# Attention on one core: first pair's transposes in another order, value units numbered from four, last head normalised in one piece

## The chip, the cores and the metric

The kernel runs on one core of a Trainium2 chip, as one launch. The metric is the device time in microseconds (us), the median of several runs. A core has five engines that run side by side, each with its own instruction stream, and that wait for one another through semaphores: TensorE (PE in the profile; its weight loads are PEld), VectorE (DVE), ScalarE (ACT), GpSimd (POOL) and SyncE (SP), which issues DMAs. TensorE writes its results into PSUM, from which ScalarE and VectorE read.

## The reference

```python
def reference(q, k, v):                      # each [8, 8, 512, 64], float32
    scale = 1.0 / np.sqrt(q.shape[-1])
    scores = np.einsum('bhqd,bhkd->bhqk', q, k) * scale
    scores = scores - scores.max(axis=-1, keepdims=True)
    attn = np.exp(scores)
    attn = attn / attn.sum(axis=-1, keepdims=True)
    return np.einsum('bhqk,bhkd->bhqd', attn, v).astype(np.float32)
```

These are 64 independent heads of softmax attention, with 512 queries, 512 keys and 64 dimensions each.

## The kernel before

**Tiling.** Heads go in pairs, 32 of them (`g` from 0 to 31). A head's keys and queries are cut into four chunks of 128. A block `(g, c, h)` is the scores of key chunk `c` of head `h` of pair `g` against all 512 queries; it is computed transposed, keys on the partitions, so that exp(scores) can be the stationary operand of the second product without another transpose. Two blocks make a group: one PSUM buffer `st` of two banks (three such buffers rotate), one exp of 128x1024 on ScalarE into an fp16 tile `pt`. The last two blocks are groups of their own (127 and 128). No maximum is subtracted.

**A pair's way.** k, q and v come by DMA from SyncE's queue. GpSimd casts them to fp16 (`cast_qk`, `cast_v`). Eight TensorE transposes of a pair (`transposes`) go into a PSUM bank, and VectorE copies the bank to `tqk` (`copy`). Two matmuls per group make the scores (`scores`), which run in half of the array's rows each. The second product is cut into units: one unit is a chunk of 128 queries of one head, four matmuls of 65 columns that accumulate over the four key chunks. The 65th column of v is one, so that the sum of the exps comes out beside the result (`values`). Seven units share one PSUM bank. When a bank is full, VectorE takes the reciprocals of the sums and multiplies (`normalise`), into an SBUF ring of 56 units, and SyncE writes each complete head out.

**Raised groups.** Six groups are not given to ScalarE: VectorE computes their exp by integer and polynomial steps (`raise_`, which reads `st`, and six `pass_` steps that read SBUF only).

**Two PSUM banks for transposes and values.** Tags `x0` and `x1` are shared by the transposes' banks and the units' banks, so whichever asks next has to wait until VectorE has read the older one.

**Order.** It is written out beforehand: `Plan` walks through time with a cost for each step (`SLOT`, `EXP`, `NORM` and so on) and emits a list of steps; the kernel then issues them in that order under a manual schedule. On TensorE, `step_pe` chooses between scores, transposes and value units; `HURRY` is the amount of exp work queued at ScalarE below which scores are issued at once. On VectorE, `step_dve` takes jobs that are due (raise first, then copies and normalisings by due time), and starts a pass of a raised group where the next job is due later than the pass's length less `LATE`. Each engine executes its own stream strictly in that order.

**Opening.** Pair 0 is handled apart (`first_loads`, `first_pair`), since nothing can start until its q and k have come. Its loads and casts are cut in halves. While they come, TensorE multiplies a matrix of ones (`busy`), six times with 512 columns and three with 128. Then: q of head 0, first half, is transposed (`tp_qa`), k of head 0, first half (`tp_ka`), q's second half (`tp_qc`), k's second half (`tp_kc`); each is copied by VectorE. Two more matmuls of ones, then the scores of the first group in two halves of 256 queries (`st_0a`, `st_0b`), k of head 1 transposed (`tp_kb`), group 1's scores, q of head 1 (`tp_qb`), one matmul of ones with 256 columns, group 2's scores. From group 3 on the plan takes over.

**End.** The last head of pair 31 is not in units: as each of its four key chunks has its exp, `last_values` adds that chunk to all four query chunks. Before the change these four lie in two places, two query chunks each (a bank and one of the three score buffers), the exp of the last block is cut in two halves of 256 queries, and each half is normalised and written out by itself, one through SyncE's queue and one through ScalarE's.

Of the kernel before, what the change touches and what calls it, by code (L numbers as in the profile page):

```python
# [8 lines left out]
FP32 = mybir.dt.float32  # L9
# [7 lines left out]
class Plan:  # L17
# [10 lines left out]

    SLOT, EXP, EXP_DONE, EXP_FIXED = 216, 853, 1085, 51
# [4 lines left out]
    RAISE, PASSES, LATE = 1216, (867, 822, 1400, 1400, 1400, 1372), 500  # L34
    HURRY = 1100
    STEP = 5

    def __init__(self, groups, pairs, first):
# [14 lines left out]
        self.units = 0  # L53
# [74 lines left out]

    def values(self, t):
        if self.head is None:  # L130
# [5 lines left out]
            if self.units % 7 == 0 and self.bank(t) is None:  # L136
                return False
# [5 lines left out]
        if self.units % 7 == 0:  # L143
            n = self.bank(t)
            if n is None:
                return False
            self.banks[n] = 1e9
            self.bank_v = n
        self.note(t, "values", g, h, part, self.units, self.bank_v)
        self.full(t, self.V_UNIT)  # L150
        self.units += 1
        last = (g, h) == (self.pairs - 1, 1)
        if self.units % 7 == 0 and not last:
            self.ready.append((self.pe + self.TO_DVE, "norm", (self.units - 7, 7, self.bank_v)))
# [66 lines left out]
def kernel(  # L221
# [128 lines left out]
    def scores(m, on_dve):  # L350
# [19 lines left out]
        if m == len(groups) - 1:  # L370
            pt2 = ppool.tile([P, 2, S], FP16, tag="pt", name="pt_last")
            blocks[grp[0]] = (pt[:, 0, :], pt2[:, 0, :])
            for n, t in enumerate((pt, pt2)):
                q2 = slice(256 * n, 256 * n + 256)
                nc.scalar.activation(out=t[:, 0, q2], in_=st[:, 0, q2], func=EXP, scale=scale)
            return
# [58 lines left out]
    def normalise(u, n):  # L435
        o = os[u // 7]
        rc = opool.tile([P, 7, 1], FP32, tag="rc", name=f"rc_{u}")
        nc.vector.reciprocal(out=rc[:, 0:n], in_=o[:, 0:n, D : D + 1])  # L438
        nc.vector.tensor_tensor(  # L439
            out=ring[:, u % NU : u % NU + n, :],  # L440
            in0=o[:, 0:n, 0:D],
# [9 lines left out]
    def values(g, h, y, u, bank):  # L451
# [5 lines left out]
        if u % 7 == 0:  # L457
# [10 lines left out]
    def last_values(c, bank):  # L468


        if c == 0:
            last["o"] = [
                ps_x.tile([P, 7, D + 1], FP32, tag=f"x{bank}", name="o_last_0"),
                ps_st.tile([P, 2, S], FP32, tag="st", name="o_last_1")[:, 0, 0 : 2 * D + 2].rearrange(
                    "p (n d) -> p n d", n=2
                ),
            ]
            last["ob"] = [opool.tile([P, 2, D], FP32, tag="obl", name=f"obl_{n}") for n in range(2)]
        for n in range(2):
            o, ob = last["o"][n], last["ob"][n]  # L480
            for x in range(2):
# [177 lines left out]
```

## Time and profile before

The profile is one execution of the program.

| | before |
|---|---|
| median of 5 runs | 124.22 us (124.0 to 124.27) |
| the profiled execution | 124.27 us, of which the span is 122.5 us |
| ScalarE busy | 114.4 us (93% of the span), 128 instructions |
| TensorE busy | 108.1 us (88%), 1562 matmuls |
| VectorE busy | 98.2 us (80%), 159 instructions |
| GpSimd busy | 70.5 us (58%) |
| DMA | 33.81 MB, 276 GB/s on average |

The span is cut into 40 equal slices of about 3.06 us; a digit is the busy share of a slice in tenths:

```profile
PE   7979698899899899989899798899988899898960
DVE  0455989799979989989999988978998699798460
ACT  4499999999999999999999999999999999999950
DMA  3899999999999969989999999999999933222234
```

Three lines are at or near nine tenths through the middle, so the shares alone don't tell which engine sets the pace. A row of costliest groups reads: line of the kernel, engine, operation, written tile <- read tiles with their shapes, count | busy us in total, mean ns of one | idle us of the engine just before them, and what ended most of it. A timeline row reads: start in us, us, engine, line, operation, tiles, count, and in brackets the idle time before it and what ended it. Rows of the timeline join several instructions of a kind; their ends overlap[...].

### The profile page before, as it was taken

The page shows a single profiled execution, that of the slowest core. Times are in us where ns is not written, and L with a number is a line of the kernel's source. Part 1 is how long each engine was busy: PE and PEld are TensorE (multiplying, and loading weights), DVE is VectorE, ACT ScalarE, POOL GpSimd, SP SyncE. Part 2 cuts the span into 40 slices and gives each one's busy share as a digit, 9 for nine tenths or more (in the row PEclk, how much of TensorE's full clock was granted, in tenths as well). Part 3 has the DMA queues.
Part 4 walks back from the last instruction along what each step waited for, and adds up shares of the span by engine and source line. Part 5 has one row for each costly group of instructions (what it writes and reads, how often), then busy time and mean ns, then how long its engine had stood idle before and what let it go on. Part 6 is the DMA issues. An engine that isn't in the chain of part 4 may idle for free.

```text
span 122.5 us, 3961 instructions
## 1 busy us (share of the span) xinstructions
PE 108.1 (88%) x1562; PEld 67.1 (55%) x1562; DVE 98.2 (80%) x159; ACT 114.4 (93%) x128; POOL 70.5 (58%) x113
## 2 busy tenths in 40 slices
PE   7979698899899899989899798899988899898960
PEld 2446265555565556565466555466645475565640
DVE  0455989799979989989999988978998699798460
ACT  4499999999999999999999999999999999999950
POOL 3269779999694635877967745476584690000000
PEclk9999999999999999999999999999999999999999
DMA  3899999999999969989999999999999933222234
GB/s 108 282 350 382 385 377 383 382 325 282 365 316 318 296 213 296 326 280 315 331 360 312 292 335 321 280 314 375 323 289 340 351 100 126 86 92 88 93 126 128
DMA packets 35602, 33.81 MB, mean 276 GB/s; under 512 B 2688, under 2 KB 35584, under 8 KB 35584
## 3 DMA queue, kind: packets, MB, share of 16 engines
q1 hardware_dynamic: 35152, 33.24, 82.1%
q10 hardware_dynamic: 432, 0.33, 0.8%
q8 instruction: 12, 0.20, 0.7%
q14 instruction: 6, 0.05, 0.2%
HBM read 25.17 MB, written 8.39 MB: 274 GB/s over the span
## 4 chain that ended last, share of the span: by engine, by line
ACT 54%; PE 27%; issue 14%; DVE 2%; ACTq 0%
ACT pt L377 54%; PE st L365 10%; PE o L460 10%; PE tp L339 3%; PE st_0a L516 3%; DVE tqk L344 1%; PE st L551 1%; DVE ring L439 1%; DVE obl L497 0%; DVE qt L594 0%; PE tp_qb L546 0%; PE tp_qc L546 0%; PE tp_qa L546 0%; PE st_0a L551 0%; PE tp_kb L540 0%
## 5 line engine op out<-in xcount | busy, mean ns | idle before, releaser
L377 ACT ACTIVATE pt<-st 128x1024 f16<-128x1024 f32 (+1 forms) x119 | 108.9, 1271 | 0.1
L365 PE MATMUL st<-tqk 64*128 64x512 f16 x248 | 47.8, 384 | 6.8 <-ACT pt L377 4.7
L460 PE MATMUL o<-vp,pt 128*128 128x65 f16 x1008 | 47.8, 195 | 2.0 <-ACT pt L377 1.9
L460 PEld LDWEIGHTS <-pt 128*128 128x128 f16 x1008 | 37.6, 98 | 19.0 <-issue 14.7
L322 POOL CAST qkp<-k 128x512 f16<-128x512 f32 x31 | 21.7, 699 | 24.3 <-DMA k<-in_k_dram 13.6
L314 POOL CAST vp<-v 128x512 f16<-128x512 f32 x32 | 27.3, 853 | 0.9 <-DMA v<-in_v_dram 0.7
L346 DVE COPY tqk<-tp 128x1024 f16<-128x1024 f16 x30 | 20.6, 688 | 5.8 <-PE tp L339 5.5
L322 POOL CAST qkp<-q 128x512 f16<-128x512 f32 x30 | 22.4, 748 | 3.2 <-DMA q<-in_q_dram 2.7
L365 PEld LDWEIGHTS <-tqk 64*128 64x128 f16 x248 | 12.9, 93 | 19.9 <-issue 11.6
L439 DVE TENSOR_TENSOR ring<-o,rc 128x448 f32<-128x448 f32 x36 | 22.5, 624 | 1.2
L339 PE MATMUL tp<-ident,qkp 128*128 128x128 f16 x248 | 19.7, 220 | 0.5 <-DVE ring L439 0.4
L339 PEld LDWEIGHTS <-qkp 128*128 128x128 f16 x248 | 14.1, 98 | 7.6 <-issue 4.8
L426 DVE SCALAR_TENSOR_TENSOR y<-y,m 128x1024 f32<-128x1024 f32 x12 | 15.7, 1308 | 0.0
L438 DVE RECIPROCAL rc<-o 128x7 f32<-128x7 f32 x36 | 7.2, 200 | 7.6 <-PE o L460 7.1
L426 DVE SCALAR_TENSOR_TENSOR pt<-y,e 128x1024 f16<-128x1024 f32 x6 | 8.4, 1403 | 0.0
L426 DVE SCALAR_TENSOR_TENSOR y<-m 128x1024 f32<-128x1024 f32 x6 | 8.2, 1358 | 0.0
L391 DVE TENSOR_SCALAR z<-st 128x1024 uint32<-128x1024 f32 x6 | 7.3, 1221 | 0.5 <-PE st L365 0.2
L404 DVE TENSOR_SCALAR m<-z 128x1024 uint32<-128x1024 uint32 x6 | 5.5, 909 | 0.0
L415 DVE TENSOR_SCALAR e<-z 128x1024 uint32<-128x1024 uint32 x6 | 4.5, 754 | 0.0
L516 PE MATMUL st_0a<-const-bfloat16-1.0 128*128 128x512 bf16 (+1 forms) x11 | 3.5, 482 | 0.8 <-PEq L643 0.8
L526 DVE CAST q<-q 128x128 f16<-128x128 f32 x1 | 0.2, 227 | 3.3 <-DMA q<-in_q_dram 3.3
L528 ACT ACT_TABLE_LOAD x1 | 1.3, 1283 | 1.7 <-PEq L643 1.7
(47 smaller groups left out, 20.8 us busy)
## 6 DMA issues: line engine op xcount, KB each, us to landing
out_dram<-ring SPq DMA_DIRECT2D x63, 128.0 KB, 3.9
k<-in_k_dram SPq DMA_DIRECT2D x31, 256.0 KB, 4.7
q<-in_q_dram SPq DMA_DIRECT2D x31, 256.0 KB, 4.9
v<-in_v_dram SPq DMA_DIRECT2D x27, 256.0 KB, 5.2
v<-in_v_dram SPq DMA_DIRECT2D x10, 128.0 KB, 4.6
k<-in_k_dram ACTq DMA_DIRECT2D x2, 128.0 KB, 2.8
q<-in_q_dram SPq DMA_DIRECT2D x2, 128.0 KB, 2.6
out_dram<-obl ACTq DMA_DIRECT2D x1, 64.0 KB, 1.6
```

The costliest lines, as they stand in the source:

```text
L314: nc.gpsimd.tensor_copy(out=vps[g % NV][:, :, :, 0:D], in_=raw[g]["v"][:, :, :, :])
L322: eng.tensor_copy(out=t[:, n].rearrange("p i (h d) -> p h i d", h=2), in_=raw[g][name][:, :, :, :],)
L339: nc.tensor.transpose(tps[g][:, n, i, :], qkp[g][:, n, i, :], ident)
L346: nc.vector.tensor_copy(out=tqk[g][:, :, :], in_=tps.pop(g).rearrange("p n i c -> p n (i c)"))
L365: nc.tensor.matmul(st[:, x, :], kc, qc, start=True, stop=True)
L377: nc.scalar.activation(out=pt[:, 0:size, :], in_=st[:, 0:size, :], func=EXP, scale=scale)
L391: nc.vector.tensor_scalar(out=r["z"][:, :, :], in0=r["st"][:, :, :], scalar1=scale * 1.4426950408889634 * 2.0**23, scalar2=(127 + SHIFT) * ...
L426: nc.vector.scalar_tensor_tensor(out=r["pt"][:, :, :] if n == 3 else r["y"][:, :, :], in0=mant if n == 0 else r["y"][:, :, :], scalar=QUAR ...
L438: nc.vector.reciprocal(out=rc[:, 0:n], in_=o[:, 0:n, D : D + 1])
L439: nc.vector.tensor_tensor(out=ring[:, u % NU : u % NU + n, :], in0=o[:, 0:n, 0:D], in1=rc[:, 0:n].broadcast_to([P, n, D]), op=AluOp.mult,)
L460: nc.tensor.matmul(os[u // 7][:, u % 7, :], blocks[(g, c, h)][:, y * P : (y + 1) * P], vps[g % NV][:, h, c, :], start=(c == 0), stop=(c == ...
L516: nc.tensor.matmul(dst[:, 0:n], ones[:, 0:P], ones[:, 0:n], start=True, stop=True)
```

## The change

- **Opening.** One of the three short matmuls of ones goes. The eight transposes of head 1's q (`tp_qb`) move ahead of the first scores; the transpose of k's second half (now into a part of group 1's own score buffer, as is `tp_qc`) moves from ahead of the first scores to between their two halves. The two matmuls of ones now stand ahead of group 1's scores, and the one with 256 columns ahead of group 2's is replaced by five with 128. The copies follow in the same new order; q of head 1 is copied before k of head 1.
- **Units.** Numbering starts at 4 (`FIRST_UNIT`), so the first bank holds three units, and every bank's border lies four units earlier in the order of heads. A bank also ends before the last head, so that there is a last piece of four units. `edge` says where a bank begins and ends, `normalise` takes the offset within the bank.
- **Plan's constants.** `LATE` 500 to 700, `HURRY` 1100 to 1200. With these and the units the order of all later steps comes out differently; the groups raised on VectorE were 6, 24, 43, 62, 82 and 102, and are 6, 23, 42, 62, 80 and 101.
- **End.** The last block's exp is one instruction of 512 queries. The last head's four query chunks lie in one bank, which is normalised by one reciprocal and one multiply; two DMAs still write the result, by SyncE's and ScalarE's queue.

```diff
--- before.py
+++ after.py
@@ -26,14 +26,17 @@
...
     SLOT, EXP, EXP_DONE, EXP_FIXED = 216, 853, 1085, 51
     INTO, OUT_OF = 95, 105
     TRANSPOSE, V_UNIT = 225, 130
     TO_ACT, TO_DVE, TO_PE = 275, 210, 60
     COPY, NORM, NORM_COLUMN = 700, 380, 67
-    RAISE, PASSES, LATE = 1216, (867, 822, 1400, 1400, 1400, 1372), 500
-    HURRY = 1100
+    RAISE, PASSES, LATE = 1216, (867, 822, 1400, 1400, 1400, 1372), 700
+    HURRY = 1200
     STEP = 5
+    FIRST_UNIT = 4
 
     def __init__(self, groups, pairs, first):
         self.groups, self.pairs = groups, pairs
@@ -50,7 +53,7 @@
         self.banks = [5100, 5800]
         self.todo = [(g, h) for g in range(pairs) for h in range(2)]
         self.head = None
-        self.units = 0
+        self.units = self.FIRST_UNIT
         self.member = {b: m for m, grp in enumerate(groups) for b in grp}
         self.ready = []
         self.passes = []
@@ -126,6 +129,11 @@
         chunks = (part,) if (g, h) == (self.pairs - 1, 1) else range(4)
         return max(self.exps.get(self.member[(g, c, h)], 1e9) for c in chunks)
 
+    def edge(self):
+
+        u, first = self.units, self.FIRST_UNIT
+        return u % 7 == 0 or u in (first, first + 8 * self.pairs - 4)
+
     def values(self, t):
         if self.head is None:
             for g, h in self.todo[:14]:
@@ -133,25 +141,26 @@
                     break
             else:
                 return False
-            if self.units % 7 == 0 and self.bank(t) is None:
+            if self.edge() and self.bank(t) is None:
                 return False
             self.todo.remove((g, h))
             self.head = (g, h, 0)
         g, h, part = self.head
         if t < self.wants(g, h, part):
             return False
-        if self.units % 7 == 0:
+        if self.edge():
             n = self.bank(t)
             if n is None:
                 return False
             self.banks[n] = 1e9
             self.bank_v = n
+            self.begun = self.units
         self.note(t, "values", g, h, part, self.units, self.bank_v)
         self.full(t, self.V_UNIT)
         self.units += 1
-        last = (g, h) == (self.pairs - 1, 1)
-        if self.units % 7 == 0 and not last:
-            self.ready.append((self.pe + self.TO_DVE, "norm", (self.units - 7, 7, self.bank_v)))
+        if self.edge() and (g, h) != (self.pairs - 1, 1):
+            what = (self.begun, self.units - self.begun, self.bank_v)
+            self.ready.append((self.pe + self.TO_DVE, "norm", what))
         self.head = (g, h, part + 1) if part < 3 else None
         return True
 
@@ -367,13 +376,6 @@
         if on_dve:
             raised[m] = {"st": st, "pt": pt}
             return
-        if m == len(groups) - 1:
-            pt2 = ppool.tile([P, 2, S], FP16, tag="pt", name="pt_last")
-            blocks[grp[0]] = (pt[:, 0, :], pt2[:, 0, :])
-            for n, t in enumerate((pt, pt2)):
-                q2 = slice(256 * n, 256 * n + 256)
-                nc.scalar.activation(out=t[:, 0, q2], in_=st[:, 0, q2], func=EXP, scale=scale)
-            return
         nc.scalar.activation(
             out=pt[:, 0:size, :], in_=st[:, 0:size, :], func=EXP, scale=scale
         )
@@ -433,12 +435,12 @@
         )
 
     def normalise(u, n):
-        o = os[u // 7]
+        o, x = os[u // 7], u % 7
         rc = opool.tile([P, 7, 1], FP32, tag="rc", name=f"rc_{u}")
-        nc.vector.reciprocal(out=rc[:, 0:n], in_=o[:, 0:n, D : D + 1])
+        nc.vector.reciprocal(out=rc[:, 0:n], in_=o[:, x : x + n, D : D + 1])
         nc.vector.tensor_tensor(
             out=ring[:, u % NU : u % NU + n, :],
-            in0=o[:, 0:n, 0:D],
+            in0=o[:, x : x + n, 0:D],
             in1=rc[:, 0:n].broadcast_to([P, n, D]),
             op=AluOp.mult,
         )
@@ -454,7 +456,7 @@
             return last_values(y, bank)
         if y == 0:
             heads.append((g, h, u))
-        if u % 7 == 0:
+        if u // 7 not in os:
             os[u // 7] = ps_x.tile([P, 7, D + 1], FP32, tag=f"x{bank}", name=f"o_{u // 7}")
         for c in range(NI):
             nc.tensor.matmul(
@@ -469,39 +471,31 @@
 
 
         if c == 0:
-            last["o"] = [
-                ps_x.tile([P, 7, D + 1], FP32, tag=f"x{bank}", name="o_last_0"),
-                ps_st.tile([P, 2, S], FP32, tag="st", name="o_last_1")[:, 0, 0 : 2 * D + 2].rearrange(
-                    "p (n d) -> p n d", n=2
-                ),
-            ]
-            last["ob"] = [opool.tile([P, 2, D], FP32, tag="obl", name=f"obl_{n}") for n in range(2)]
-        for n in range(2):
-            o, ob = last["o"][n], last["ob"][n]
-            for x in range(2):
-                qc = 2 * n + x
-                b = blocks[(LAST, c, 1)]
-                b = b[n] if c == NI - 1 else b
-                nc.tensor.matmul(
-                    o[:, x, :],
-                    b[:, qc * P : (qc + 1) * P],
-                    vps[LAST % NV][:, 1, c, :],
-                    start=(c == 0 and x == 0),
-                    stop=(c == NI - 1),
-                    skip_group_check=True,
-                )
-            if c < NI - 1:
-                continue
-            rc = opool.tile([P, 7, 1], FP32, tag="rc", name=f"rc_last_{n}")
-            nc.vector.reciprocal(out=rc[:, 0:2], in_=o[:, 0:2, D : D + 1])
-            nc.vector.tensor_tensor(
-                out=ob[:, :, :],
-                in0=o[:, 0:2, 0:D],
-                in1=rc[:, 0:2].broadcast_to([P, 2, D]),
-                op=AluOp.mult,
-            )
-            (nc.sync, nc.scalar)[n].dma_start(
-                out=source(out, LAST)[:, 1, 2 * n : 2 * n + 2], in_=ob[:, :, :]
+            last["o"] = ps_x.tile([P, 7, D + 1], FP32, tag=f"x{bank}", name="o_last")
+        o = last["o"]
+        for x in range(NI):
+            nc.tensor.matmul(
+                o[:, x, :],
+                blocks[(LAST, c, 1)][:, x * P : (x + 1) * P],
+                vps[LAST % NV][:, 1, c, :],
+                start=(c == 0 and x == 0),
+                stop=(c == NI - 1),
+                skip_group_check=True,
+            )
+        if c < NI - 1:
+            return
+        ob = opool.tile([P, NI, D], FP32, tag="obl", name="obl")
+        rc = opool.tile([P, 7, 1], FP32, tag="rc", name="rc_last")
+        nc.vector.reciprocal(out=rc[:, 0:NI], in_=o[:, 0:NI, D : D + 1])
+        nc.vector.tensor_tensor(
+            out=ob[:, :, :],
+            in0=o[:, 0:NI, 0:D],
+            in1=rc[:, 0:NI].broadcast_to([P, NI, D]),
+            op=AluOp.mult,
+        )
+        for n, queue in enumerate((nc.sync, nc.scalar)):
+            queue.dma_start(
+                out=source(out, LAST)[:, 1, 2 * n : 2 * n + 2], in_=ob[:, 2 * n : 2 * n + 2, :]
             )
 
     def first_loads():
@@ -530,11 +524,16 @@
         nc.scalar.copy(k16[:, 1], tk[:, 1])
         nc.gpsimd.tensor_copy(out=q16[:, 1], in_=tq[:, 1])
 
-        st0 = ps_st.tile([P, 2, S], FP32, tag="st", name="st_0a")
-        pk0 = ps_st.tile([P, 2, 8, P], FP16, tag="st", name="tp_ka")
-        pk1 = ps_st.tile([P, 2, 8, P], FP16, tag="st", name="tp_kc")
-        pq0 = ps_x.tile([P, 8, P], FP16, tag="x0", name="tp_qa")
-        pq1 = ps_x.tile([P, 8, P], FP16, tag="x1", name="tp_qc")
+        st0, pka, st1 = (
+            ps_st.tile([P, 2, S], FP32, tag="st", name=f"st_{n}") for n in ("0a", "ka", "1")
+        )
+        pqa = ps_x.tile([P, 8, P], FP16, tag="x0", name="tp_qa")
+        pqb = ps_x.tile([P, 8, P], FP16, tag="x1", name="tp_qb")
+
+        pka, pkc, pqc = pka[:, 0, :], st1[:, 0, :], st1[:, 1, :]
+        pka, pkc, pqc = (
+            t.bitcast(FP16).rearrange("p (n c) -> p n c", c=P) for t in (pka, pkc, pqc)
+        )
 
         def t_k(dst, h, j):
             nc.tensor.transpose(
@@ -561,39 +560,38 @@
 
         for n in range(6):
             busy(st0[:, 0], S)
-        for n in range(3):
+        for n in range(2):
             busy(st0[:, 0], P)
         for i in range(2):
-            t_q(pq0[:, i], 0, i)
-        nc.vector.tensor_copy(out=qt[:, 0, 0:2], in_=pq0[:, 0:2])
-        t_k(pk0[:, 0, 0], 0, 0)
-        nc.vector.tensor_copy(out=kt[:, 0, 0], in_=pk0[:, 0, 0])
+            t_q(pqa[:, i], 0, i)
+        nc.vector.tensor_copy(out=qt[:, 0, 0:2], in_=pqa[:, 0:2])
+        t_k(pka[:, 0], 0, 0)
+        nc.vector.tensor_copy(out=kt[:, 0, 0], in_=pka[:, 0])
         for i in range(2):
-            t_q(pq1[:, i], 0, 2 + i)
-        nc.vector.tensor_copy(out=qt[:, 0, 2:4], in_=pq1[:, 0:2])
-        t_k(pk1[:, 0, 0], 0, 1)
-        nc.vector.tensor_copy(out=kt[:, 0, 1], in_=pk1[:, 0, 0])
-        for n in range(2):
-            busy(st0[:, 0], P)
+            t_q(pqc[:, i], 0, 2 + i)
+        nc.vector.tensor_copy(out=qt[:, 0, 2:4], in_=pqc[:, 0:2])
+        for i in range(NI):
+            t_q(pqb[:, i], 1, i)
         pts = [ppool.tile([P, 2, S], FP16, tag="pt", name=f"pt_{m}") for m in range(3)]
         for m in range(3):
             for x, b in enumerate(groups[m]):
                 blocks[b] = pts[m][:, x, :]
         first_scores(st0, 0, 0, 0, 256, pts[0], 0, 256)
+        t_k(pkc[:, 0], 0, 1)
+        nc.vector.tensor_copy(out=kt[:, 0, 1], in_=pkc[:, 0])
+        nc.vector.tensor_copy(out=qt[:, 1], in_=pqb[:, 0:4])
         st0b = ps_st.tile([P, 2, S], FP32, tag="st", name="st_0b")
         first_scores(st0b, 0, 0, 256, 512, pts[0], 0, 256)
+        for n in range(2):
+            busy(st1[:, 1], P)
+        first_scores(st1, 0, 1, 0, S, pts[1], 0, S)
         pkb = ps_x.tile([P, 8, P], FP16, tag="x0", name="tp_kb")
         for j in range(2):
             t_k(pkb[:, j], 1, j)
         nc.vector.tensor_copy(out=kt[:, 1], in_=pkb[:, 0:2])
-        st1 = ps_st.tile([P, 2, S], FP32, tag="st", name="st_1")
-        first_scores(st1, 0, 1, 0, S, pts[1], 0, S)
-        pqb = ps_x.tile([P, 8, P], FP16, tag="x1", name="tp_qb")
-        for i in range(NI):
-            t_q(pqb[:, i], 1, i)
-        nc.vector.tensor_copy(out=qt[:, 1], in_=pqb[:, 0:4])
         st2 = ps_st.tile([P, 2, S], FP32, tag="st", name="st_2")
-        busy(st2[:, 0], 256)
+        for n in range(5):
+            busy(st2[:, 0], P)
         first_scores(st2, 1, 0, 0, S, pts[2], 0, S)
         first.update(kt=kt, qt=qt)
 
```

## The prediction, made before the changed kernel was run

> **What bounds the kernel now.** I read the table of costliest groups first, then the timeline of ScalarE (start, length, what, count, idle before it), then the timeline of all engines at both ends.
>
> ```profile
> L377 ACT ACTIVATE pt<-st 128x1024 f16<-128x1024 f32 (+1 forms) x119 | 108.9, 1271 | 0.1
> ```
>
> The exps of the planned part leave ScalarE idle for 0.1 us in 109. So TensorE's 108.1 us, VectorE's 98.2 us and the loads matter only where they make an exp late.
>
> ```profile
> 5.54 0.60 ACT L558 ACTIVATE pt<-st_0a 128x512 f16<-128x512 f32 x1 [0.97 <-PE st_0a L551]
> 6.04 0.59 ACT L558 ACTIVATE pt<-st_0b 128x512 f16<-128x512 f32 x1
> 6.51 2.17 ACT L558 ACTIVATE pt<-st 128x1024 f16<-128x1024 f32 x2
> 8.57 2.11 ACT L377 ACTIVATE pt<-st 128x1024 f16<-128x1024 f32 x2
> ...
> 114.70 2.88 ACT L377 ACTIVATE pt<-st 128x1024 f16<-128x1024 f32 x3
> 116.98 0.88 ACT L375 ACTIVATE pt<-st 128x256 f16<-128x256 f32 x1
> 117.25 0.89 ACT L375 ACTIVATE pt_last<-st 128x256 f16<-128x256 f32 x1
> ```
>
> Taken one by one, two full exps follow each other by 0.904 us in their starts but by 0.917 in their ends, and the ends are what other engines wait for. The exp that starts at 9.66 ends at 10.68, and 116 full exps later one ends at 117.09: 106.41/116 = 0.917. Only two ends in between come late, by 0.05 us (at 45.6) and 0.04 us (at 48.3). So the middle is rigid, a start may slip by its gathered lead (12.5 ns an exp) at no cost, and the change can move three things: the end at 10.68, those 0.08 us, and all that follows 117.09.
>
> The opening:
>
> ```profile
> 5.97 0.39 PE L551 MATMUL st<-qt,kt 64*128 64x512 f16 x2
> 6.29 0.41 PE L546 MATMUL tp_qb<-ident,q 128*64 128x128 f16 x8
> 6.75 0.42 DVE L594 COPY qt<-tp_qb 128x512 f16<-128x512 f16 x1 [0.38 <-PE tp_qb L546]
> 7.22 0.39 PE L551 MATMUL st<-qt,kt 64*128 64x512 f16 x2 [0.30 <-DVE qt L594]
> 8.42 0.76 DVE L344 COPY tqk<-tp 128x512 f16<-128x512 f16 x2 [0.92 <-PE tp L339]
> 9.23 0.39 PE L365 MATMUL st<-tqk 64*128 64x512 f16 x2 [0.61 <-DVE tqk L344]
> ```
>
> The fourth exp (7.65) and the sixth (9.66) start late: each waits for scores that waited for a copy on VectorE. The end:
>
> ```profile
> 116.65 1.11 PE L460 MATMUL o<-vp,pt 128*128 128x65 f16 x24
> 117.60 0.59 PE L485 MATMUL o_last<-vp,pt 128*128 128x65 f16 x14
> 117.80 0.21 DVE L438 RECIPROCAL rc<-o 128x7 f32<-128x7 f32 x1 [1.05 <-PE o L460]
> 118.04 0.62 DVE L439 TENSOR_TENSOR ring<-o,rc 128x448 f32<-128x448 f32 x1
> 118.19 0.23 PE L485 MATMUL o_last<-vp,pt_last 128*128 128x65 f16 x2
> 118.58 0.16 DVE L496 RECIPROCAL rc_last<-o_last 128x2 f32<-128x2 f32 x1
> 119.18 0.29 DVE L497 TENSOR_TENSOR obl<-o_last,rc_last 128x128 f32<-128x128 f32 x1
> 119.50 0.37 ACTq L503 DMA_DIRECT2D out_dram<-obl  x1
> 119.59 0.40 SPq L503 DMA_DIRECT2D out_dram<-obl  x1
> ```
>
> Here VectorE bounds, not the last exp: the bank of units 245 to 251 closes only with the next-to-last head, its normalising (117.80 to 118.66) stands before the last head's two pieces, and the last piece ends at 119.47.
>
> **What the Trainium skill says.** "TensorE: Matmul & The Clock Gate", Part 1, "What's actually happening": the array runs at half rate until it has been busy for one free-running window of about 3.4 us. The trace agrees: ones-matmuls of 128 columns are 107 ns apart at 3.3 us, transposes 56 ns apart at 7.8; the switch falls between 5.7 and 6.3. "Perfetto Trace Analysis", "DVE / Act Engine Instruction": a row ends when the write is acknowledged and the semaphore pushed, which is why I count exps by ends. "DMA: Bandwidth & Descriptors", "Anatomy of one DMA": about 2 us fixed for a transfer; the last two take 1.6 and 1.8 us here, so only their issue time can move.
>
> **The change, part by part.** Its waits are read from the built program's order. From the trace before: a change of matmul form costs 0.24 us from the last 128-column start to the next load (0.35 after 256 columns at half rate, 0.16 and 0.31 at full rate after 128 and 512), the end of an operation reaches TensorE 0.05 us later, and scores reach their exp 0.43 us after they start.
>
> *Opening.* One short ones-matmul goes (0.107), so tp_qa starts at 3.63 instead of 3.74 (its cast ends at 3.53). tp_ka 3.99, tp_qc 4.21 and 4.32, then the eight moved transposes (four pairs, 0.107 each) 4.42 to 4.74; their cast on GpSimd ends at 4.31, which just covers them. Out of that stretch go the kc transpose with its two form changes and two ones-matmuls. First scores 4.99 (before 5.10), first exp 5.43 (5.54). The kc transpose now stands between the halves: 5.34, then second scores 5.59 (5.29), exp 6.02 (6.04): what was gained is spent. The two ones-matmuls wait for the kc copy (5.34+0.33+0.22+0.05 = 5.94), and behind them wait the third scores: 6.16 (5.97), exp 6.58 (6.51). So far +0.07. But the long qb copy (0.42) is now made before that, and the fourth scores wait for the kb copy alone: kb 6.48 and 6.54, copy 6.79 to 7.08 (0.29), scores 7.14 (7.22), exp 7.56 (7.65). The five ones-matmuls (5 x 0.056 = 0.28) end before 7.14, beside the copy. The rest follows with it: scores 3 (7.36), pair 1's transposes 7.68 (7.76), copies until 9.10 (9.18), fifth scores 9.15, sixth exp 9.57 (9.66). **-0.08**; bounds -0.15 and +0.15, as the clock's switch is free to fall elsewhere.
>
> *Middle.* The number of exps stays, six groups are still raised on VectorE (now 6, 23, 42, 62, 80, 101), and the normalised columns stay, in 37 pieces instead of 36: one more reciprocal and multiply (about 0.4 us) on an engine idle for 20%. The first piece of three waits for units 4 to 6 (9.9+0.23), ends at 10.7, and the next units want that bank at 11.0; transposes of pair 2 are copied behind it at 10.63, no later than now. Pair 3's transposes move ahead of scores 9: these start at 12.67 and their exp, due at 13.21, could start at 13.09. HURRY and LATE shift the interleaving: a VectorE pass may now hold up a due copy or normalising by 0.7 us instead of 0.5. Below: the two small gaps go, -0.08; above: the rival below, +0.7. I take **0**, since lead hid nearly everything of this kind before.
>
> *End.* Units are now numbered from 4, so the bank of 245 to 251 closes with head 1 of pair 30, before the last pair's units: after 8 of the 24 matmuls at 116.65, last start 116.89. Its reciprocal comes at 116.89+0.23 = 117.12 (before 117.80), multiply 117.36 to 117.98. The last pair's first head gets a bank and a piece of four (estimate for 256 columns from 292 ns for 128 and 624 for 448: 0.43): about 118.10 to 118.53. New wait: the 16 o_last matmuls need the bank that the multiply frees, so they start at 118.04 instead of 117.60; nothing else is queued behind them on TensorE. They last 0.46 (15 x 0.031); the undivided exp would end at 117.58+0.49 = 118.07 (the halves: 118.13), ahead of the four that need it. Reciprocal 118.50+0.23 = 118.73, multiply 118.93 to 119.36, both DMAs at 119.40. SP's three ring DMAs (118.01, 118.40, 118.80, some 0.4 each) are out by then. Against the later of the old issues, 119.59: -0.19. TensorE can gain more: scores 128 start at 116.33, while the exp that frees their buffer ended at 116.17; up to 0.11, and pair 25's old values now stand ahead of pair 29's, which cost a wait of 0.33 us at 110.7. I take half: **-0.24**; bounds -0.4 and +0.1.
>
> *Sum:* -0.08+0-0.24 = -0.32 on the profiled 124.27 us (span 122.5, 1.77 outside), 123.95; the median of the runs is 0.05 lower: **123.90**.
>
> **Rivals.**
> - *The ends give less.* The third exp's delay stays in the chain, or the 4-unit piece pushes the last one: opening 0, end -0.1, so 124.1. For: both gains hang on steps of 0.05 to 0.1 us. Against: each copy on the chain really is shorter or earlier.
> - *ScalarE starves at raised groups (slower).* A raised group holds one of three score buffers until its first pass is done, and a delayed copy delays the next scores. At group 43 two starts slipped by 0.17+0.33 = 0.50; the lead was 0.43, so 0.05 reached the ends. Where that happens early (group 23: lead about 0.2) or twice within a few groups, 0.3 to 0.5 comes through. Two such places, +0.7: 124.6. It decides from 0.57 us on. For: LATE at 700, VectorE at nine tenths from 20 to 80. Against: five of six raised groups lost nothing.
> - *TensorE runs ahead.* With no wait at 110.7 and no gaps, the end gains 0.45 and the middle 0.08: 123.6.
>
> **How the numbers follow.** Forecast 0.55 (its own range 123.65 to 124.1), less 0.22, starved 0.15, ahead 0.08. About 0.2%, 0.25 us, is what a measurement can tell: faster is below 123.97, slower above 124.47. Faster: most of the first, the last, little of the second: 0.60. Slower: most of the starved case: 0.14. The rest, 0.26, is within. The range for 8 in 10: 123.55 to 124.35.
>
> **What would show it.** First exp at 5.43, fourth 7.56, sixth 9.57; idle before the planned exps still 0.1; the last exp's end near 118.0; o_last waiting for VectorE's multiply, and its DMAs near 119.3. Wrong if exps' ends in the middle come late by more than 0.2 in sum, or if the first 10 us gain nothing.

## The result, and the profile after

| | before | after |
|---|---|---|
| median | 124.12 us (80 runs) | 124.53 us (43 runs) |
| ratio after/before | | 1.0036 (95%: 1.0024 to 1.0048) |
| profiled execution, its span | 124.27, 122.5 us | 124.20, 122.4 us |

The change makes the kernel slower by a third of a per cent. The forecast, 123.90 us and faster, is wrong in its sign, and the result lies outside its range. Yet the steps that the forecast worked out are there in the profile. The planned exps first (columns of the costliest groups):

```profile
L379 ACT ACTIVATE pt<-st 128x1024 f16<-128x1024 f32 (+1 forms) x120 | 109.4, 1328 | 0.1
```

Idle is still 0.1 us in front of ScalarE, and exp by exp no end after the sixth comes late any more (before: 0.08 us in two places). The opening, in the timeline of ScalarE and then of TensorE:

```profile
5.22 0.60 ACT L557 ACTIVATE pt<-st_0a 128x512 f16<-128x512 f32 x1 [0.74 <-PE st_0a L550]
5.71 0.59 ACT L557 ACTIVATE pt<-st_0b 128x512 f16<-128x512 f32 x1
6.29 2.02 ACT L557 ACTIVATE pt<-st 128x1024 f16<-128x1024 f32 x2
```

```profile
4.43 0.53 PE L545 MATMUL tp_qb<-ident,q 128*64 128x128 f16 x8
4.89 0.28 PE L550 MATMUL st_0a<-qt,kt 64*128 64x256 f16 x2
5.11 0.23 PE L539 MATMUL st<-ident,k 128*128 128x128 f16 x1
5.27 0.28 PE L550 MATMUL st_0b<-qt,kt 64*128 64x256 f16 x2
```

In this execution the first exp starts at 5.22 and the sixth ends at 10.31 (before: 10.68). More than the change is in that: the two 256-column matmuls of `st_0a` take 0.28 us here and took 0.40 before, so TensorE came to its full rate earlier. Two later profiles with the old opening (before with 1 and with 16 tiny instructions more on VectorE, below) have the sixth exp's end at 10.07 and 10.28 too, so the 0.37 us can't be put down to the change. The end, in the timeline of all engines:

```profile
116.58 0.21 DVE L440 RECIPROCAL rc<-o 128x7 f32<-128x7 f32 x1 [1.52 <-PE o L462]
116.82 0.62 DVE L441 TENSOR_TENSOR ring<-o,rc 128x448 f32<-128x448 f32 x1
117.36 0.17 DVE L440 RECIPROCAL rc<-o 128x4 f32<-128x4 f32 x1
...
117.50 0.67 PE L477 MATMUL o_last<-vp,pt 128*128 128x65 f16 x16 [0.19 <-DVE ring L441]
117.57 0.42 DVE L441 TENSOR_TENSOR ring<-o,rc 128x256 f32<-128x256 f32 x1
118.21 0.18 DVE L489 RECIPROCAL rc_last<-o_last 128x4 f32<-128x4 f32 x1 [0.21 <-PE o_last L477]
118.42 0.42 DVE L490 TENSOR_TENSOR obl<-o_last,rc_last 128x256 f32<-128x256 f32 x1
118.88 0.40 SPq L497 DMA_DIRECT2D out_dram<-obl  x1
118.88 0.37 ACTq L497 DMA_DIRECT2D out_dram<-obl  x1
```

Both last DMAs are issued at 118.88, where the later one was issued at 119.59: 0.71 us earlier. The span is 0.1 us shorter. So 0.6 us are lost after the last instruction that the kernel's text contains. Where, is in the list of DMA issues (queue, count, KB, us from issue to landing), before and after:

```profile
out_dram<-obl ACTq DMA_DIRECT2D x1, 64.0 KB, 1.6
out_dram<-obl SPq DMA_DIRECT2D x1, 64.0 KB, 1.8
```

```profile
out_dram<-obl SPq DMA_DIRECT2D x1, 64.0 KB, 2.7
out_dram<-obl ACTq DMA_DIRECT2D x1, 64.0 KB, 1.7
```

SyncE's output takes 0.9 us longer, and the program's end waits for it; in the waits of SyncE's queue (us, times, longest), before and after, the longest wait for it grows from 0.2 to 1.0 us:

```profile
SPq L654 <- DMA out_dram<-obl: 0.4, 2, 0.2
```

```profile
SPq L652 <- DMA out_dram<-obl: 1.3, 2, 1.0
```

The queues' table has one more hint, a kind of transfer that the kernel doesn't issue (packets, MB, share); before, then after:

```profile
q14 instruction: 6, 0.05, 0.2%
```

```profile
q14 instruction: 7, 0.06, 0.2%
```

One more instruction packet of 8 KB falls into the profiled time. The trace's DMA records (not a view of the page) show it, and what it meets:

```
after: instruction packet, 8192 bytes: starts 120.23, takes 0.466 us
       packets of the last outputs (512 bytes): 0.025 to 0.044 us each; all but four have
       ended by 120.35, these four end between 120.72 and 120.79
       landing marks of the last output: fifteen from 120.54 to 120.77, the sixteenth at 121.58
before: instruction packet, 8192 bytes: starts 123.09, when all outputs have landed (last packet's end 121.00, last mark 121.35)
```

One packet of 0.47 us among packets of 0.03 us, four output packets that end right behind it, and one landing mark of sixteen that is 0.8 us late. The packet's own length accounts for about half of this: the last mark follows the last output packet by 0.79 us here and by 0.35 before, and no run shows why. To see what else happened I cut the tail of each profiled execution into three: from the end of the last exp to the start of the last DMA issue; from there to SyncE's last wait for an output; from there to the end of the span.

| us | last exp ends | to last issue | to its wait's end | closing | tail in all |
|---|---|---|---|---|---|
| before | 118.13 | 1.46 | 1.77 | 1.12 | 4.35 |
| after | 117.62 | 1.26 | 2.72 | 0.82 | 4.79 |

The landing costs 0.95 more, the closing 0.31 less, and the end's own work 0.20 less: +0.44 together, against +0.41 in the medians. The closing is nothing but waits and drains that all engines pass together. In the records of before, VectorE's last drain begins 0.477 us after the wait ahead of it, and after the change 0.118 us:

```
VectorE, closing         wait     drain    wait
before                   121.655  122.132  122.435
after                    121.882  122.000  122.361
```

That stall in before stands ahead of the instruction packet of 123.09. So before seems to pay for the packet as well, but less, and in another place; the experiments test this.

Some executions of every kernel here are longer than its fastest by more than 1.25 us (50 of 189 with the new opening, 31 of 280 of before, 19 of 93 of the other kernels with the old opening; in the one of them that was profiled TensorE keeps its half rate until about 11 us), and medians and ratios still contain a part of these, so the tables below also give the mean without them, called the mean of the others, with its 95% interval.

### The profile page after: what moved, and what is told of

Same layout as the page of the kernel before. It is cut to its first block, busy times and chain, and to the rows that moved or that the text cites. A ratio compares the mean times of both kernels' runs of the same rounds, so it can differ in the third digit from the quotient of the medians.

```text
span 122.4 us, 3967 instructions
## 1 busy us (share of the span) xinstructions
PE 107.7 (88%) x1565; PEld 67.3 (55%) x1565; DVE 97.9 (80%) x159; ACT 114.3 (93%) x127; POOL 75.4 (62%) x113
## 4 chain that ended last, share of the span: by engine, by line
ACT 54%; PE 22%; issue 18%; DVE 2%; ACTq 0%
ACT pt L379 54%; PE st L374 8%; PE o L462 6%; PE tp L348 2%; PE st_0a L510 2%; DVE tqk L353 1%; PE st L550 1%; PE o_last L477 1%; DVE ring L441 1%; DVE obl L490 0%; PE tp_qa L545 0%; PE st L545 0%; PE tp_qb L545 0%; DVE kt L591 0%; PE st L510 0%
## 5 line engine op out<-in xcount | busy, mean ns | idle before, releaser
L462 PE MATMUL o<-vp,pt 128*128 128x65 f16 x1008 | 46.8, 195 | 1.5 <-ACT pt L379 1.3
L462 PEld LDWEIGHTS <-pt 128*128 128x128 f16 x1008 | 37.0, 98 | 18.4 <-issue 14.7
L331 POOL CAST qkp<-k 128x512 f16<-128x512 f32 x31 | 27.0, 870 | 23.3 <-DMA k<-in_k_dram 19.5
L323 POOL CAST vp<-v 128x512 f16<-128x512 f32 x32 | 26.5, 829 | 0.9 <-DMA v<-in_v_dram 0.8
L331 POOL CAST qkp<-q 128x512 f16<-128x512 f32 x30 | 23.0, 768 | 2.0 <-DMA q<-in_q_dram 1.9
L441 DVE TENSOR_TENSOR ring<-o,rc 128x448 f32<-128x448 f32 (+2 forms) x37 | 22.6, 612 | 1.3
L440 DVE RECIPROCAL rc<-o 128x7 f32<-128x7 f32 (+2 forms) x37 | 7.3, 198 | 9.8 <-PE o L462 9.8
L417 DVE TENSOR_SCALAR e<-z 128x1024 uint32<-128x1024 uint32 x6 | 5.7, 954 | 0.0
L406 DVE TENSOR_SCALAR m<-z 128x1024 uint32<-128x1024 uint32 x6 | 4.7, 784 | 0.0
L510 PEld LDWEIGHTS <-const-bfloat16-1.0 128*128 128x128 bf16 x15 | 1.6, 120 | 2.6 <-issue 2.4
```

The lines of the kernel that those rows point to most:

```text
L323: nc.gpsimd.tensor_copy(out=vps[g % NV][:, :, :, 0:D], in_=raw[g]["v"][:, :, :, :])
L331: eng.tensor_copy(out=t[:, n].rearrange("p i (h d) -> p h i d", h=2), in_=raw[g][name][:, :, :, :],)
L440: nc.vector.reciprocal(out=rc[:, 0:n], in_=o[:, x : x + n, D : D + 1])
L441: nc.vector.tensor_tensor(out=ring[:, u % NU : u % NU + n, :], in0=o[:, x : x + n, 0:D], in1=rc[:, 0:n].broadcast_to([P, n, D]), op=AluOp. ...
L462: nc.tensor.matmul(os[u // 7][:, u % 7, :], blocks[(g, c, h)][:, y * P : (y + 1) * P], vps[g % NV][:, h, c, :], start=(c == 0), stop=(c == ...
L510: nc.tensor.matmul(dst[:, 0:n], ones[:, 0:P], ones[:, 0:n], start=True, stop=True)
```

## The experiments

Theories. **F**, the fetch: VectorE's instructions come in packets of 8 KB by the same DMA engines as the data; the change leaves VectorE's stream one instruction longer (196 in the built program instead of 195, waits and drains included, of which the trace has 194 and 193 records: a 37th piece adds two and a wait, the undivided last head takes two away), and that lets the packet start among the last outputs' packets. **S**, the rival on record: ScalarE starves at raised groups. **W**: the new opening gains nothing or costs, since its moved transposes wait for a cast.

**Move the packet without touching the work.** A repetition of after; 16 tiny VectorE instructions put in at its start, where VectorE has nothing to do (the packet should come 16 instructions earlier); a ring of 112 units instead of 56, by which waits go and 188 instructions are left (the packet should come after the end); and, the other way round, one tiny instruction put into before.

```diff
+        idle = cpool.tile([P, 1], FP32, name="idle")
+        for n in range(16):
+            nc.vector.memset(idle[:, :], 0.0)
         nc.vector.tensor_copy(out=q16[:, 0, 0:2], in_=tq[:, 0, 0:2])
```

```diff
-    NU = 56
+    NU = 112
```

After again, unedited:

> The changed kernel again, unaltered, for a second profile. In its first profile the exps end 0.51 us earlier than before (117.63 against 118.13) and the last DMAs are issued at 118.88 instead of 119.59, and yet the span is only 0.1 us shorter: the last output lands 2.7 us after its issue, not 1.8, and in the DMA records an instruction fetch of 8 KB (0.47 us on one DMA engine, at 120.23) lies in front of some of its packets; before, that fetch comes at 123.1, after the end. Theory F (fetch): it comes in each execution of this program, as it hangs on VectorE's count of instructions (196 in the program, 195 before), so this profile has it again between 119 and 121.5, with a landing of 2.3 us or more; ratio to before 1.002 to 1.006. Theory S (starved): the profile was a lucky one, and this one shows late ends of exps in the middle, 0.3 us or more in sum; the fetch needn't be there.

After with 16:

> The changed kernel with 16 more tiny memsets on VectorE in its idle first microseconds (before 3 us), so that the fetch, if it is VectorE's, falls some 16 instructions earlier in its stream, around 112 to 116 us, far from the last output. Theory F: last output lands in 1.6 to 1.9 us again, ratio to before 0.995 to 0.998 (0.3 to 0.6 us faster than before). Theory S: nothing changes, ratio 1.003 to 1.005.

After with the larger ring:

> The changed kernel with an output ring of 112 units instead of 56: VectorE's multiplies wait for fewer output DMAs, which takes 8 waiting instructions off its stream (188 instead of 196). Theory F: VectorE ends short of the point at which it fetches, no fetch in the last 10 us, ratio 0.995 to 0.998. Theory S: 1.003 to 1.005, as the order on TensorE and ScalarE is the same.

Before with one (`range(1)`):

> The kernel before with one tiny memset more on VectorE in its idle first microseconds: 196 instructions like the changed kernel, nothing else. Theory F: the fetch moves from 123.1 to about 121, among the packets of the last output, which lands in 2.3 us or more; ratio to before 1.003 to 1.008. Theory S: 1.000.

| | ratio to before (95%) | mean of the others | packet starts | landing | closing | tail |
|---|---|---|---|---|---|---|
| before | | 124.05 ± 0.07 | 123.09 | 1.77 | 1.12 | 4.35 |
| after | 1.0036 (1.0024 to 1.0048) | 124.42 ± 0.10 | 120.23 | 2.72 | 0.82 | 4.79 |
| after again | 1.0024 (1.0005 to 1.0044) | 124.33 ± 0.13 | 120.36 | 2.74 | 0.82 | 4.81 |
| after, 16 more | 0.9975 (0.9951 to 0.9999) | 123.55 ± 0.10 | 111.39 | 1.86 | 0.82 | 3.93 |
| after, ring of 112 | 0.9988 (0.9961 to 1.0016) | 123.58 ± 0.14 | none in the last 13 us | 1.87 | 0.82 | 3.94 |
| before, 1 more | 1.0066 (1.0046 to 1.0085) | 124.81 ± 0.16 | 120.35 | 2.59 | 0.82 | 4.87 |

Before was run again beside each set of experiments; its mean of the others was 124.05, 124.00, 124.02 and 124.06, so rows of different sets compare within about 0.1 us.

After with 16 instructions *more* is 0.87 us faster than after (124.42 - 123.55), and before with a single one more is 0.76 us slower than before. The landing goes with the packet's place in all six rows, and the tails account for the means: against before, the two versions of after with the packet moved away have tails shorter by 0.42 and 0.41 and are faster by 0.50 and 0.47; before with one more has a tail longer by 0.52 and is slower by 0.76, with 0.28 us of late exps in its profile (before: 0.08). F is shown in both directions: that the packet's place sets the landing. S falls: moving the packet takes away the whole loss, and the profile of after has no late exp at all behind the sixth. The one number outside what F had put is the ratio of the larger ring (0.9988, put at 0.995 to 0.998). The last output of before with 1 more, in its list of DMA issues:

```profile
out_dram<-obl SPq DMA_DIRECT2D x1, 64.0 KB, 2.6
```

The list of DMA issues of after with 16 more:

```profile
out_dram<-obl SPq DMA_DIRECT2D x1, 64.0 KB, 1.8
out_dram<-obl ACTq DMA_DIRECT2D x1, 64.0 KB, 1.7
```

The timeline of VectorE in the same run shows where the packet is asked for:

```profile
110.23 0.21 DVE L440 RECIPROCAL rc<-o 128x7 f32<-128x7 f32 x1
110.70 0.62 DVE L441 TENSOR_TENSOR ring<-o,rc 128x448 f32<-128x448 f32 x1 [0.27 <-DVE rc L440]
112.07 0.20 DVE L440 RECIPROCAL rc<-o 128x7 f32<-128x7 f32 x1 [0.74 <-PE o L462]
```

The multiplies at the end follow their reciprocals at once (116.58 and 116.82 above, 118.21 and 118.42); here there are 0.27 us of idle time that nothing explains, 0.7 us before the packet at 111.39. Counted in the records, waits and drains included, this multiply is VectorE's 192nd of the run. The 192nd record is the drain of the closing in before, and the wait ahead of that drain in after (121.882 in the table above), which has to wait for the other engines anyway: no stall can be seen there, but the packet falls among the outputs'.

**The packet a little earlier.** F as I had put it says that only a packet among the last outputs' own costs. Four instructions more instead of 16:

```diff
-        for n in range(16):
+        for n in range(4):
```

> The changed kernel with 4 tiny idle memsets on VectorE: the fetch should move four VectorE instructions ahead of where the changed kernel has it, that is to about 1.3 us behind the start of the piece of four (117.4), so to 118.6 or 119, among the ring's packets and just ahead of the last output's. Theory F: no or little delay of the last output (landing 1.6 to 2.1 us), ratio 0.996 to 1.000. If any fetch in the last microseconds costs the same: 1.002 or more.

Ratio 1.0047 (1.0019 to 1.0075), mean of the others 124.27 ± 0.18: as slow as after, and the expectation is missed. The packet started at 118.44, before the last outputs were even issued. VectorE's timeline, and the last issues with their landing:

```profile
117.32 0.17 DVE L440 RECIPROCAL rc<-o 128x4 f32<-128x4 f32 x1
117.76 0.42 DVE L441 TENSOR_TENSOR ring<-o,rc 128x256 f32<-128x256 f32 x1 [0.26 <-DVE rc L440]
```

```profile
out_dram<-obl SPq DMA_DIRECT2D x1, 64.0 KB, 2.5
out_dram<-obl ACTq DMA_DIRECT2D x1, 64.0 KB, 2.3
```

The stall is again at the 192nd record. It costs no time by itself (the issue is at 118.83, as with 16 more: 118.81), but both outputs land late; of the last one's landing marks fifteen lie between 120.47 and 120.65 and one at 121.34. The same is seen in each of the four transfers that land ahead of it: one mark of sixteen comes 0.7 to 1.1 us behind the other fifteen, and with 16 more none does. That fits one DMA engine of sixteen that carried the packet of 0.68 us and stayed behind. From which distance it costs nothing lies between this (0.4 us ahead of the issue) and 16 more (7.4 us ahead); it wasn't tried closer.

**The parts alone.** Before with the new opening only, twice (in the first profile TensorE kept its half rate until about 11 us); before with the new end only; before with the units and constants only; after with before's constants; after with before's opening; and before with nothing but the 16 instructions, as the control for those that have them.

```diff
         for n in range(6):
             busy(st0[:, 0], S)
-        for n in range(3):
+        for n in range(2):
             busy(st0[:, 0], P)
...
+        for i in range(NI):
+            t_q(pqb[:, i], 1, i)
```

> The kernel before with the changed opening alone (195 instructions on VectorE, so no early fetch). Theory F with the sums on record: the exps start earlier and the rest follows, -0.08 us by the sum, up to -0.4 if TensorE reaches full clock before the first scores, as in all five profiles of changed kernels or later runs so far; ratio 0.997 to 0.9995. Theory P (the plan's gaps eat it): sixth exp's end earlier, but as much more in late ends of exps, ratio 1.000.

> The kernel before with the changed opening alone, again, since in its first profile the eight moved transposes waited for GpSimd's cast of head 1's q (they start at 4.87, not 4.42) and TensorE stayed at half rate until about 11 us. Theory O (the opening is worth its sum): a profile with the sixth exp's end at 10.6 or earlier and ratio 0.997 to 0.9995. Theory W (the moved transposes wait for the cast often enough to eat the gain): the transposes start after 4.5 here too, ratio 1.000 to 1.003.

The end only (the rest of `last_values` as in the change):

```diff
-        if m == len(groups) - 1:
-            pt2 = ppool.tile([P, 2, S], FP16, tag="pt", name="pt_last")
...
+            last["o"] = ps_x.tile([P, 7, D + 1], FP32, tag=f"x{bank}", name="o_last")
```

> The kernel before with the undivided last exp and the last head in one piece, nothing else (193 instructions on VectorE, no early fetch). Its bank of units 245 to 251 still closes with the next-to-last head, so the multiply of seven still stands ahead of the last piece: one reciprocal and a multiply of 0.42 us instead of two of each, 0.81 to 0.89 us from the first reciprocal to the end before and about 0.6 us now. Sum on record applied to this alone: -0.15 to -0.25 us, ratio 0.998 to 0.999. Theory P: 1.000, the end being set by the ring's DMAs.

Units from four and the constants only, with 16:

```diff
-    RAISE, PASSES, LATE = 1216, (867, 822, 1400, 1400, 1400, 1372), 500
-    HURRY = 1100
+    RAISE, PASSES, LATE = 1216, (867, 822, 1400, 1400, 1400, 1372), 700
+    HURRY = 1200
     STEP = 5
+    FIRST_UNIT = 4
```

> The kernel before with units numbered from 4 and the two constants of the plan, its own opening and end, and 16 idle memsets on VectorE that keep the fetch off the end. Theory F: about -0.1 us or nothing, as the bank of 245 to 251 closes earlier but two pieces follow; ratio 0.998 to 1.001. Theory S: the new order starves ScalarE, late ends of exps 0.3 us or more, 1.003 or more.

After with 16 and the constants of before:

```diff
-    RAISE, PASSES, LATE = 1216, (867, 822, 1400, 1400, 1400, 1372), 700
-    HURRY = 1200
+    RAISE, PASSES, LATE = 1216, (867, 822, 1400, 1400, 1400, 1372), 500
+    HURRY = 1100
```

> The changed kernel with the old LATE and HURRY (500, 1100) and the 16 idle memsets: beside the changed kernel with the memsets (0.9975) it shows what the constants are worth. Theory F: the lead hides their work, 0.997 to 0.999. Theory S: the new constants cost something, so this is faster still, 0.995.

After with 16 and the opening of before:

```diff
-        for n in range(2):
+        for n in range(3):
             busy(st0[:, 0], P)
...
-        for i in range(NI):
-            t_q(pqb[:, i], 1, i)
```

> The changed kernel with the old opening and 16 idle memsets on VectorE that keep the fetch off the end. Theory O: slower than the changed kernel with the memsets (0.9975) by about 0.1 us, ratio 0.998 to 0.9995. Theory W: as fast or faster, 0.995 to 0.9975.

Before with 16:

> The control: the kernel before with 16 idle memsets on VectorE, so with a fetch near 112 us instead of behind the end. Theory F: 0.999 to 1.001, as neither the memsets nor a fetch away from the last output cost anything; then the gain of the changed kernel with the memsets is the change's own. If the memsets themselves make a kernel faster, this is below 0.998.

| | ratio to before (95%) | mean of the others | to issue | landing | closing | tail |
|---|---|---|---|---|---|---|
| before, new opening | 1.0017 (0.9996 to 1.0038) | 124.02 ± 0.11 | 1.46 | 1.78 | 1.12 | 4.35 |
| the same again | 1.0038 (1.0009 to 1.0067) | 124.13 ± 0.17 | 1.46 | 1.75 | 1.12 | 4.33 |
| before, new end | 0.9987 (0.9968 to 1.0006) | 123.81 ± 0.15 | 1.52 | 1.75 | 0.82 | 4.10 |
| before, 16 | 0.9983 (0.9956 to 1.0009) | 123.69 ± 0.10 | 1.46 | 1.75 | 0.82 | 4.03 |
| before, units and constants, 16 | 0.9982 (0.9956 to 1.0007) | 123.55 ± 0.14 | 1.39 | 1.65 | 0.82 | 3.85 |
| after, old constants, 16 | 1.0007 (0.9979 to 1.0035) | 123.76 ± 0.14 | 1.45 | 1.85 | 0.82 | 4.12 |
| after, old opening, 16 | 0.9958 (0.9941 to 0.9975) | 123.48 ± 0.14 | 1.26 | 1.84 | 0.82 | 3.92 |

*The control* is 0.36 ± 0.12 us faster than before in the means, by 16 instructions more. Its closing is 0.82 instead of 1.12, which gives 0.30 of it: before pays for the packet in its closing, which F had not put (its 0.999 to 1.001 is missed by the ratio, 0.9983, though not by its interval). Three profiles have VectorE's stream of 195 (before and the two with the new opening), and these three alone have a closing of 1.12; all others have 0.82, among them four without tiny instructions (after twice, the larger ring and the new end), so it isn't the tiny instructions themselves. *The end alone* has 193 instructions, and its gain of 0.24 ± 0.17 is the closing's 0.30 too; its issue comes no earlier (1.52). In its timeline:

```profile
116.72 2.73 SPq L440 DMA_DIRECT2D out_dram<-ring  x4
...
117.98 0.62 DVE L432 TENSOR_TENSOR ring<-o,rc 128x448 f32<-128x448 f32 x1
118.53 0.17 DVE L480 RECIPROCAL rc_last<-o_last 128x4 f32<-128x4 f32 x1
118.73 0.42 DVE L481 TENSOR_TENSOR obl<-o_last,rc_last 128x256 f32<-128x256 f32 x1
119.19 0.35 ACTq L488 DMA_DIRECT2D out_dram<-obl  x1
119.54 0.40 SPq L488 DMA_DIRECT2D out_dram<-obl  x1
```

Without the units from four the bank of seven is still multiplied until 118.60, so the head that it completes comes late to SyncE, whose four DMAs from the ring last until 119.45, and SyncE's half of the last output stands behind them until 119.54, though VectorE is done at 119.15. *Units and constants* alone are 0.14 ± 0.17 us faster than the control, which can't be told from nothing; no exp behind the sixth comes late. *The constants* were put at nothing or at a small loss, and the ratio of that run, 1.0007, is above both forecasts, though its interval reaches F's: with the old ones after with 16 is 0.21 ± 0.17 us slower. In the profile the end shows it: the bank's multiply came at 117.08 to 117.70 with the last exp ending at 117.70 as well (after: 116.82 to 117.44, and 117.62), and to the issue it is 1.45. So by these profiles, one for each, the 0.2 us of the end need all three: units, constants and one piece.

*The opening* changes the time by -0.03 ± 0.13 and +0.08 ± 0.18 us in the means: nothing that can be told. Against the full version with 16 the old opening is 0.07 ± 0.17 faster. What its moved transposes wait for is seen in the first of these runs, whose load of head 1's q came late, in the timeline of GpSimd and of TensorE:

```profile
4.42 0.40 POOL L531 CAST q<-q 128x256 f16<-128x256 f32 x1 [0.42 <-DMA q<-in_q_dram]
```

```profile
7.41 0.74 PE L516 MATMUL st<-const-bfloat16-1.0 128*128 128x128 bf16 x5
```

The cast ends at 4.82 instead of 4.31, the transposes start at 4.87, and the first scores, which don't need them, at 5.44. This profile also has TensorE at half rate (five ones-matmuls take 0.74 us, after the change 0.45). In the other one the cast began at 3.80 and the first exp at 5.05, but the cast of pair 1's keys waited 2.82 us for its load and ended at 7.63 (before: 6.95), and the sixth exp ended at 10.82. So theory O (the opening is worth its sum) is missed, and of W only its result holds, no gain that can be measured: its reason, the wait for the cast, is in the first profile alone (in the second the transposes started at 4.40). Whether the new opening makes TensorE's long half rate more frequent, which would cost something in the medians and ratios, stays open; the counts given with the result lean that way.

*After with the old opening and 16 instructions* beats both kernels: 0.42% faster than before (0.25% to 0.59%).

## Why the prediction was wrong

- **The step that failed:** "the last two take 1.6 and 1.8 us here, so only their issue time can move". The landing moved from 1.77 to 2.72 us: +0.95 that the sum didn't have. I had carried one execution's landing over as a constant. The Trainium skill ("DMA: Bandwidth & Descriptors", "Anatomy of one DMA") gives a fixed part of about 2 us that scales with nothing, but for transfers by GpSimd's path; these go by SyncE's and ScalarE's queues, and in these runs their landing is no constant: without a packet near them the landings of the profiles lie between 1.65 and 1.87, with a packet they are 2.52 to 2.74.
- **A term that was missing, with the other sign:** what lies behind the last landing was taken as fixed, too. It fell by 0.31 (1.12 to 0.82), because VectorE's 192nd record was no longer the drain that the other engines wait for. I had counted the VectorE instructions that the change adds by their duration only ("one more reciprocal and multiply (about 0.4 us) on an engine idle for 20%"), not by their place in the stream.
- **Opening, -0.08:** each time in the list was met within 0.01 us or beaten (first exp 5.43 forecast, 5.22 found; fourth 7.56 and 7.29), but that is in part luck: the forecast took TensorE's full rate to begin where it did before, and in this execution it began ahead of the first scores. By the runs of the opening alone it is 0 within about 0.15, inside the bounds given. The cast that "just covers" the transposes is no sure cover: it began between 3.80 and 4.42 in the profiles of these runs.
- **Middle, 0:** right. ScalarE stayed rigid, no exp late, and the two gaps, 0.08 together, closed, which had been named as the lower bound. The starvation rival, 0.15 of the chance and the only one on the slow side, has nothing for it.
- **End, -0.24:** by its own measure right: from the end of the last exp of 128x1024 to the last issue 2.24 us instead of 2.50, so -0.26 (0.06 of it from the undivided exp, the rest behind the last exp); the new wait of `o_last` on the bank (0.19 us idle, ended by VectorE's multiply) came as put. But two outputs issued at the same time land 0.1 us later than two that are issued 0.1 us apart (1.84 to 1.87 against 1.75 to 1.78), so about 0.16 of it arrives.
- **The sum:** after against before with the packet far from both (16 more in each) is -0.14 ± 0.14 us, where -0.32 was forecast. The sign forecast was that of the work, though its interval just reaches zero; with the packet, -0.14 + 0.86 (its landing, 2.72 against 1.86) - 0.31 (the closing) = +0.41. That this is exactly the difference of the medians is luck, as -0.14 alone is uncertain by as much; the means differ by 0.37 ± 0.12.

## What to carry to other kernels

Here one instruction packet delayed the last output by 0.7 to 0.9 us. So a forecast of an end needs a line for each transfer there, those included that the kernel doesn't issue: look at the instruction packets in the queues' table, and at when they start. If a change that shortens the path makes the kernel slower, put in some idle instructions on the engine whose count changed before you judge the change: here 16 of them were worth 0.87 us, while 4 moved the packet too little. And measure parts on top of such a control, or a part that merely changes the count looks like a gain, as the new end alone did.

## What the runs showed of the hardware

I had not expected that an engine's instruction packets could reach the time at all. They travel as packets of 8 KB (of 16 KB in the other instruction queue, which the table lists as q8) that took 0.31 to 1.1 us each, against 0.025 to 0.047 us for an output's packets at the end. VectorE's started 0.8 to 1.4 us after the end of its 191st record in all thirteen profiles that have so many; with the larger ring VectorE has 186 records, and none of its packets is on record near the end. Where the 192nd record had nothing else to wait for, it started late: by 0.37 us in the three profiles in which it is the closing's drain, and by 0.08 to 0.24 in the six in which it is a multiply. That the packet is VectorE's is shown by moving VectorE's count alone; that it delays the output by sharing a DMA engine with it is concluded from the single late landing mark of sixteen (with 4 more in five transfers one after the other), as the records don't name the engine.
